# Feed-forward: four intermediate results of each unit stay in PSUM banks instead of SBUF tiles

## The chip, the cores and the metric

The kernel runs on one core of a Trainium2 chip. The core has five engines with a queue each: TensorE (PE in the profile) multiplies matrices into PSUM, VectorE (DVE) and ScalarE (ACT) work element by element on SBUF and PSUM, GpSimd (POOL) works element by element on SBUF, and SyncE (SP) issues the DMAs. An engine takes its instructions in the order in which they stand; engines wait for each other through semaphores. The metric is the time of one execution on the device in microseconds (us), as the median of several runs; lower is better.

## The reference

One layer of a diffusion transformer on 1024 latent tokens of width 1024. The change touches only the last part, the feed-forward, whose inner width is 4096:

```python
def squared_relu_mlp(h, w1, b1, w2, b2):
    return jnp.square(jax.nn.relu(h @ w1 + b1)) @ w2 + b2
...
        hx = modulate(rmsnorm(x_mid, g_norm_mlp[l]), sh2, sc2)
        x = x_mid + gt2 * squared_relu_mlp(hx, w_ff1[l], b_ff1[l], w_ff2[l], b_ff2[l])
```

## The kernel before

Activations are kept with features on the 128 partitions and 512 tokens (one half, `hf` 0 or 1) along a row, so one fp32 tile of 128 x 512 fills one of the eight PSUM banks. For precision every operand of a matmul is split into an upper and a lower part (`hi` by a ScalarE copy, `lo` by a subtraction on VectorE for activations and on GpSimd for weights), and three matmuls make one product.

The 4096 inner rows are worked in 16 units of 256. A unit has two row blocks of 128 and two halves of tokens, hence four hidden tiles: 11 and 12 (first block, token halves 0 and 1), 21 and 22 (second block). From unit 2 on both layers use a seven-product scheme for a 2 x 2 block product. In the first layer (`q_pieces`) the weights of a unit are a11, a12, a21, a22 and the sums s1 to s4 made of them; the token side was combined once before the loop. Seven products, of two pieces each, go in the order a11, a12, s1, s2, s3, s4, a22 into three kinds of banks: `qa` (two buffers), `qb` and `qc` (one each). One unit uses one buffer of each kind. While a bank goes on accumulating, its partial results are taken out: `new` copies a bank into an SBUF tile `ft`, `more` adds a bank to such a tile and applies bias, relu and square (`act`), `begin_21` applies them to the bank qa into a fresh tile. The hidden values come in the order 11, 22, 12, 21.

The second layer (`pair_pieces`) needs the values 11, 22 and 21 and four combinations: t1 = 12 - 11, t3 = 22 - 12, t2 = 22 - t1, t4 = 21 - t2. `sums` makes the first three, `sum_21` the last, each in place in a tile `ft`. `part` (`h_split`) makes the upper and lower parts of each, as `fh` and `fl` or `th` and `tl`. This stretch, from the sum that completes 12 to the last split, is called the tail of a unit here; it occurs in units 2 to 14, 13 times. Unit 15 ends the loop and needs the plain values only.

The products of the second layer go into `fa` (two buffers), `fb` and `fc`, and `add_x` (L1498) adds each, times a gate, to the residual `X`. Within a pair of output blocks the bank `fa` is read twice: after its first product, and again after t2's product has been accumulated onto it.

The order of TensorE, ScalarE, VectorE and GpSimd in the loop is the order in which the code is emitted (`manual_schedule`). `Pieces.emit` walks a list of pieces; it prepares weights `AHEAD` = 5 pieces in advance and puts the `post` functions behind the piece they belong to, or one or more pieces later. The first pieces of the next unit's first layer (a11, both parts, and a12) stand on TensorE between a unit's a22 and its second layer, and so do the tail's instructions on ScalarE and VectorE.

Waits are put in by the framework, from what each instruction reads and writes. Two engines that touch the same PSUM bank are kept apart also when both only read it.

Of the kernel before, what the change touches and what calls it, by code (L numbers as in the profile page):

```python
# [12 lines left out]
ALU = mybir.AluOpType  # L13
# [36 lines left out]
def body(tc, A, out, dbg=None):  # L50
    nc = tc.nc
    V, S, G, PE, SP = nc.vector, nc.scalar, nc.gpsimd, nc.tensor, nc.sync
# [37 lines left out]
    def ps_tile(tag, name, n=512):  # L90
        return cur["pool"].tile([P, n], F32, name=name, tag=tag, bufs=cur["tags"][tag])
# [23 lines left out]
    def CF(name, i=0, n=1):  # L115
        o, w = COLS[name]
        return colf[:, o - NCOLS + 40 + i:o - NCOLS + 40 + i + n]
# [157 lines left out]
    st = ExitStack()  # L275
# [572 lines left out]
    for m in range(2):  # L848
        t = q4("eo")
# [606 lines left out]
    def w_split(a):  # L1456

        n = a.shape[1]
        hi, lo = [wf.tile([P, 2, P], F32R, name=s, tag=s, bufs=6)[:, :n] for s in ("w2h", "w2l")]
        S.activation(hi, a, AF.Copy)  # L1460
        G.tensor_tensor(lo, a, hi.bitcast(F32), ALU.subtract)  # L1461
        return hi, lo

    def w1_load(f, i):
        r = wf.tile([P, 4, P], F32, name="w1r", tag="w1r", bufs=4)
        SP.dma_start(r, A["w_ff1"][f, :, 4 * i:4 * i + 4])
        return r
# [7 lines left out]
    def mm3w(o, w, i, m, start, stop):  # L1475
        for j, (a_, m_) in enumerate(((w[0], m[0]), (w[0], m[1]), (w[1], m[0]))):
            PE.matmul(o, a_[:, i, :], m_, start=start and j == 0, stop=stop and j == 2, skip_group_check=True)  # L1477

    def f_tile():
        return fin.tile([P, H], F32, name="ft", tag="ft", bufs=4)  # L1480

    def act(t, f, src=None):

        S.activation(t, t if src is None else src, AF.Relu, bias=CF("b_ff1", f))  # L1484
        S.activation(t, t, AF.Square)

    def h_split(t, extra=False):
        if extra:
            hi, lo = [th_p.tile([P, H], F32R, name=s, tag=s, bufs=3) for s in ("th", "tl")]
        else:  # L1490
            hi, lo = [fin.tile([P, H], F32R, name=s, tag=s, bufs=4) for s in ("fh", "fl")]
        S.activation(hi, t, AF.Copy)  # L1492
        V.tensor_tensor(lo, t, hi.bitcast(F32), ALU.subtract)  # L1493
        return hi, lo
# [92 lines left out]
    def q_pieces(u):  # L1587

        ts, d = {}, {}
        units[u] = d  # L1590
        st = {}

        def load(i):
            if u + 1 < NU2:
                raws.setdefault(u + 1, []).append(w1_load(2 * u + 2 + i // 2, i % 2))

        def bank(tag):
            if tag not in st:
                st[tag] = ps_tile(tag, tag)
            return st[tag]  # L1600

        def prep(name, h):
            def fn():
                a11, a12, a21, a22 = raws[u]
                if h == 0 and name == "s1":
                    st["ws"] = wf.tile([P, 4, P], F32, name="ws", tag="ws", bufs=1)
                ws = st.get("ws")
                if h == 0:
                    if name == "s1":
                        ES.tensor_tensor(ws, a21, a22, ALU.add)  # L1610
                    elif name == "s2":
                        ES.tensor_tensor(ws, ws, a11, ALU.subtract)
                    elif name == "s3":
                        ES.tensor_tensor(a21, a11, a21, ALU.subtract)  # L1614
                    elif name == "s4":
                        ES.tensor_tensor(ws, a12, ws, ALU.subtract)
                a = {"a11": a11, "a12": a12, "a22": a22, "s3": a21}.get(name, ws)
                w = w_split(a[:, 2 * h:2 * h + 2])
                if h == 0 and name == "s4":
                    for i in range(3):  # L1620
                        load(i)
                if h == 1 and name == "a22":
                    load(3)
                return w
            return fn

        def new(i, bank_):
            ts[i] = f_tile()
            S.copy(ts[i], bank_)  # L1629

        def more(i, bank_, also=None):
            V.tensor_tensor(ts[i], ts[i], bank_, ALU.add)  # L1632
            if also:
                also()
            act(ts[i], 2 * u + i // 20)

        def part(key, i, extra=False):
            d[key] = h_split(ts[i], extra)

        def sums():  # L1640
            V.tensor_tensor(ts[11], ts[12], ts[11], ALU.subtract)
            V.tensor_tensor(ts[12], ts[22], ts[12], ALU.subtract)
            V.tensor_tensor(ts[22], ts[22], ts[11], ALU.subtract)

        def begin_21():
            ts[21] = f_tile()
            act(ts[21], 2 * u + 1, st["qa"])

        def sum_21():
            V.tensor_tensor(ts[21], ts[21], ts[22], ALU.subtract)  # L1650

        post_q1 = (lambda: new(11, st["qa"]),)
        post_q2 = (lambda: more(11, st["qc"]),)
        post_q5 = (lambda: new(22, st["qb"]),)
        post_q6 = (lambda: new(12, st["qa"]),)
        pre_q7 = (lambda: part((0, 0), 11),)
        post_q7 = (lambda: more(22, st["qa"]),)
        if u == NU2 - 1:
            post_q3 = (lambda: more(12, st["qb"]), lambda: part((1, 1), 22), lambda: part((0, 1), 12))
            post_q4 = (begin_21, lambda: part((1, 0), 21))  # L1660
        else:
            post_q3 = (lambda: more(12, st["qb"], lambda: part((1, 1), 22)), sums)
            post_q4 = (lambda: (begin_21(), part("t1", 11)), lambda: (part((1, 0), 21), part("t2", 22, True)),
                       lambda: (sum_21(), part("t3", 12, True)), lambda: part("t4", 21, True))

        def piece(name, tag, b, start, h, post):
            def mm(w):
                o = bank(tag)
                for k in range(2):
                    mm3w(o, w, k, b[2 * h + k], start and h == 0 and k == 0, h == 1 and k == 1)  # L1670
            pc.entry((u, name, h), prep(name, h))
            return lambda: pc.add((u, name, h), mm, post if h == 1 else pre_q7 if name == "s3" else None)

        return [piece(*x[:4], h, x[4]) for x in (
            ("a11", "qa", b11, True, post_q1), ("a12", "qc", b21, True, post_q2), ("s1", "qb", c1, True, post_q5),
            ("s2", "qa", c2, False, post_q6), ("s3", "qa", c3, False, post_q7), ("s4", "qb", b22, False, post_q3),
            ("a22", "qa", c4, False, post_q4)) for h in range(2)]
# [95 lines left out]
    with tc.manual_schedule(engines=MAN):  # L1773
        for u in range(2, NU2):
            q = q_pieces(u)
            for _ in range(4 if u == 2 else 3):
                q.pop(0)()
            (plain_pieces if u == 2 else pair_pieces)(u - 1, q)
            for f in q:
                f()  # L1780
        pc.emit(AHEAD)
# [157 lines left out]
```

## Time and profile before

| | |
|---|---|
| median of 3 runs | 1326.41 us (1323.22 to 1332.71) |
| the profiled execution | 1320.52 us |
| its span, first to last instruction | 1318.4 us |
| TensorE matmuls busy | 1182.3 us, 90% |
| VectorE busy | 1025.8 us, 78% |
| GpSimd busy | 799.6 us, 61% |
| ScalarE busy | 650.7 us, 49% |
| mean granted clock of TensorE | 0.958 of full speed |

A busy share is a mean over the whole execution. Where an engine holds the others up is read from the waits and the timelines, which give for each instruction its start, its length and what ended the idle time ahead of it. Starts in one timeline can overlap a little, since an engine begins an instruction before the last one has quite ended. In the timelines a row with xN stands for N instructions in a row.

### The profile page before, as it was taken

The page shows a single profiled execution, that of the slowest core. Times are in us where ns is not written, and L with a number is a line of the kernel's source. Part 1 is how long each engine was busy: PE and PEld are TensorE (multiplying, and loading weights), DVE is VectorE, ACT ScalarE, POOL GpSimd, SP SyncE. Part 2 cuts the span into 40 slices and gives each one's busy share as a digit, 9 for nine tenths or more (in the row PEclk, how much of TensorE's full clock was granted, in tenths as well). Part 3 has the DMA queues.
Part 4 walks back from the last instruction along what each step waited for, and adds up shares of the span by engine and source line. Part 5 has one row for each costly group of instructions (what it writes and reads, how often), then busy time and mean ns, then how long its engine had stood idle before and what let it go on. Part 6 is the DMA issues. An engine that isn't in the chain of part 4 may idle for free.

```text
span 1318.4 us, 18813 instructions
## 1 busy us (share of the span) xinstructions
PE 1182.3 (90%) x6252; PEld 961.2 (73%) x6252; DVE 1025.8 (78%) x1604; ACT 650.7 (49%) x1335; POOL 799.6 (61%) x1004
## 2 busy tenths in 40 slices
PE   5997888997847889999989999999999999999995
PEld 3775667876636777877778787777877777877775
DVE  4657898599997857669794678888889888788877
ACT  5344334223255646555654454555544555545565
POOL 2147786472556642123566588777877777777764
PEclk9988998998876999999999999999999999999998
DMA  9554341251173554233120111111120111111113
GB/s 347 177 173 147 107 128 54 95 182 40 40 226 95 155 159 112 98 97 112 48 73 33 40 65 57 32 50 55 65 64 33 49 57 56 64 35 46 56 41 128
DMA packets 75058, 121.75 MB, mean 92 GB/s; under 512 B 16977, under 2 KB 35154, under 8 KB 74962
## 3 DMA queue, kind: packets, MB, share of 16 engines
q1 hardware_dynamic: 62802, 113.22, 26.6%
q10 hardware_dynamic: 12160, 7.34, 1.8%
q8 instruction: 49, 0.80, 0.3%
q14 instruction: 47, 0.39, 0.1%
HBM read 106.66 MB, written 13.88 MB: 91 GB/s over the span
## 4 chain that ended last, share of the span: by engine, by line
PE 52%; DVE 27%; ACT 5%; POOL 3%; DMA 3%; issue 3%; SPq 1%; ACTq 0%; DVEq 0%; POOLq 0%
PE fa L1477 11%; PE qa L1477 6%; PE qb L1477 6%; PE fb L1477 5%; DVE cacc L1020 3%; DVE tl L1493 3%; PE fc L1477 2%; PE p_t L1275 2%; PE mm L1102 2%; DVE fl L1493 2%; PE mm L364 2%; PE mm L1477 2%; DVE X L1498 1%; PE p_t L1263 1%; PE f L1477 1%
## 5 line engine op out<-in xcount | busy, mean ns | idle before, releaser
L1461 POOL TENSOR_TENSOR w2l<-w2r,w2h 128x128 fp32r<-128x128 f32 (+1 forms) x232 | 176.8, 763 | 68.8 <-ACT w2h L1460 61.1
L1498 DVE SCALAR_TENSOR_TENSOR X<-fa,gt2c,X 128x512 f32<-128x512 f32 x216 | 159.4, 745 | 13.9 <-PE fa L1477 13.9
L1460 ACT ACTIVATE w2h<-w2r 128x128 fp32r<-128x128 f32 (+1 forms) x232 | 86.1, 388 | 142.7 <-POOL w2r L1711 78.1
L235 POOL TENSOR_TENSOR wlo<-wraw,whi 128x1024 fp32r<-128x1024 f32 x30 | 74.3, 2479 | 124.0 <-ACT whi L233 118.2
L1461 POOL TENSOR_TENSOR w2l<-w1r,w2h 128x256 fp32r<-128x256 f32 x136 | 108.9, 817 | 61.2 <-ACT w2h L1460 34.4
L1498 DVE SCALAR_TENSOR_TENSOR X<-fb,gt2c,X 128x512 f32<-128x512 f32 x108 | 80.5, 745 | 36.5 <-PE fb L1477 36.0
L1461 POOL TENSOR_TENSOR w2l<-ws,w2h 128x256 fp32r<-128x256 f32 x84 | 67.9, 815 | 41.4 <-ACT w2h L1460 41.4
L1020 DVE SCALAR_TENSOR_TENSOR cacc<-cv,wdw,cacc 128x512 f32<-128x512 f32 x92 | 85.1, 971 | 0.4
L1477 PE MATMUL fa<-th,w2h 128*128 128x512 f32 x156 | 63.2, 405 | 19.7 <-DVE X L1498 19.7
L364 PE MATMUL mm<-xh,whi 128*128 128x512 f32 x192 | 77.1, 418 | 3.6 <-ACT xh L218 2.7
L364 PE MATMUL mm<-xl,whi 128*128 128x512 f32 x192 | 78.9, 411 | 0.5 <-DVE xl L220 0.5
L1460 ACT ACTIVATE w2h<-w1r 128x256 fp32r<-128x256 f32 x136 | 54.1, 410 | 48.7 <-DVE w1r L1614 19.1
L364 PE MATMUL mm<-xh,wlo 128*128 128x512 f32 x192 | 77.8, 407 | 0.0
L1477 PE MATMUL qa<-cb,w2h 128*128 128x512 f32 x224 | 70.6, 396 | 0.7 <-ACT ft L1629 0.7
L1493 DVE TENSOR_TENSOR fl<-ft,fh 128x512 fp32r<-128x512 f32 x64 | 56.1, 893 | 11.9 <-ACT fh L1492 11.3
L1477 PE MATMUL fa<-th,w2l 128*128 128x512 f32 x156 | 61.4, 394 | 0.8 <-POOL w2l L1461 0.8
L1477 PE MATMUL fa<-tl,w2h 128*128 128x512 f32 x156 | 61.5, 394 | 0.0
L1018 POOL TENSOR_TENSOR pacc<-pacc,ptmp 128x512 f32<-128x512 f32 x24 | 41.0, 1708 | 25.4 <-ACT ptmp L1017 25.4
L1460 ACT ACTIVATE w2h<-ws 128x256 fp32r<-128x256 f32 x84 | 33.2, 411 | 41.4 <-DVE ws L1610 20.7
L1477 PEld LDWEIGHTS fa<-th,w2h 128*128 128x128 f32 x156 | 29.3, 188 | 31.0 <-DVE X L1498 25.2
L1477 PEld LDWEIGHTS qa<-cb,w2h 128*128 128x128 f32 x224 | 42.0, 188 | 11.3 <-ACT ft L1629 1.1
L1484 ACT ACTIVATE ft<-ft,colf 128x512 f32<-128x512 f32 x42 | 30.5, 727 | 35.4 <-DVE ft L1632 35.4
(787 smaller groups left out, 3893.0 us busy)
## 6 DMA issues: line engine op xcount, KB each, us to landing
w2r<-in_w_ff SPq DMA_DIRECT2D x68, 256.0 KB
wmB<-in_wmodB SPq DMA_DIRECT2D x32, 512.0 KB
w1r<-in_w_ff SPq DMA_DIRECT2D x64, 256.0 KB
wm<-in_wmodA SPq DMA_DIRECT2D x16, 512.0 KB
wraw<-in_w_in SPq DMA_DIRECT2D x12, 512.0 KB
x<-in_xT SPq DMA_DIRECT2D x8, 512.0 KB
wraw<-in_w_out SPq DMA_DIRECT2D x8, 512.0 KB
kr<-k_d SPq DMA_DIRECT2D x16, 256.0 KB
```

The costliest lines, as they stand in the source:

```text
L235: (lo_eng or G).tensor_tensor(lo, raw, hi.bitcast(F32), ALU.subtract)
L364: PE.matmul(o, a_[:, k, :], b_[hf][k], start=k == 0 and i == 0, stop=k == 7 and i == 2)
L1018: G.tensor_tensor(pacc, pacc, t, ALU.add)
L1020: V.scalar_tensor_tensor(acc, x(k), w(k), acc, ALU.mult, ALU.add)
L1102: PE.matmul(o, a_[:, 2 * kk + c, :], b_, start=c == 0 and i == 0, stop=c == 1 and i == 2)
L1275: PE.matmul(po[:, j * 64:j * 64 + 64], ptt[:, i * P:(i + 1) * P], rv, start=i == 0, stop=i == 4, skip_group_check=True)
L1460: S.activation(hi, a, AF.Copy)
L1461: G.tensor_tensor(lo, a, hi.bitcast(F32), ALU.subtract)
L1477: PE.matmul(o, a_[:, i, :], m_, start=start and j == 0, stop=stop and j == 2, skip_group_check=True)
L1484: S.activation(t, t if src is None else src, AF.Relu, bias=CF("b_ff1", f))
L1493: V.tensor_tensor(lo, t, hi.bitcast(F32), ALU.subtract)
L1498: return V.scalar_tensor_tensor(x, o, gt2(k), x, ALU.mult, ALU.add).ins
```

## The change

Three results stay in the unit's own banks, and a fourth value is made in one:

- `more(12, ..., keep=True)`: the sum that completes value 12 is written back into the bank qb, and relu and square run in place there; later t3 takes its place in qb.
- `sums`: the first difference, t1, is written into the bank qc, which has been empty since value 11 took its content.
- `begin_21`: relu and square of value 21 run in place in the bank qa; later t4 takes its place in qa.

Unit 15 keeps its 12 in SBUF, and only its 21 in the bank.

```diff
-        def more(i, bank_, also=None):
-            V.tensor_tensor(ts[i], ts[i], bank_, ALU.add)
+        def more(i, bank_, also=None, keep=False):
+
+            t, ts[i] = ts[i], bank_ if keep else ts[i]
+            V.tensor_tensor(ts[i], t, bank_, ALU.add)
             if also:
                 also()
             act(ts[i], 2 * u + i // 20)
...
         def sums():
-            V.tensor_tensor(ts[11], ts[12], ts[11], ALU.subtract)
+            V.tensor_tensor(st["qc"], ts[12], ts[11], ALU.subtract)
+            ts[11] = st["qc"]
             V.tensor_tensor(ts[12], ts[22], ts[12], ALU.subtract)
             V.tensor_tensor(ts[22], ts[22], ts[11], ALU.subtract)

         def begin_21():
-            ts[21] = f_tile()
-            act(ts[21], 2 * u + 1, st["qa"])
+            ts[21] = st["qa"]
+            act(ts[21], 2 * u + 1)
...
-            post_q3 = (lambda: more(12, st["qb"], lambda: part((1, 1), 22)), sums)
+            post_q3 = (lambda: more(12, st["qb"], lambda: part((1, 1), 22), True), sums)
```

Line numbers behind `more` move by two or three. On VectorE the tail keeps its order, and the operands change. The difference of the two programs at the tail of unit 2 (- before, + changed):

```order
-L1632 TENSOR_TENSOR ft<-ft,qa 128x512
-L1632 TENSOR_TENSOR ft<-ft,qb 128x512
-L1493 TENSOR_TENSOR fl<-ft,fh 128x512
-L1641 TENSOR_TENSOR ft<-ft 128x512
-L1642 TENSOR_TENSOR ft<-ft 128x512
-L1643 TENSOR_TENSOR ft<-ft 128x512
+L1634 TENSOR_TENSOR ft<-ft,qa 128x512
+L1634 TENSOR_TENSOR qb<-ft,qb 128x512
+L1493 TENSOR_TENSOR fl<-ft,fh 128x512
+L1643 TENSOR_TENSOR qc<-qb,ft 128x512
+L1645 TENSOR_TENSOR qb<-ft,qb 128x512
+L1646 TENSOR_TENSOR ft<-ft,qc 128x512
```

L1641 to L1643 become L1643, L1645 and L1646, one for one; nothing moves. On ScalarE, in the same tail (`w2h` are upper parts of weights for later pieces):

```order
-L1484 ACTIVATE ft<-ft,colf 128x512
-L1485 ACTIVATE ft<-ft 128x512
-L1460 ACTIVATE w2h<-w2r 128x256
-L1460 ACTIVATE w2h<-w1r 128x256
-L1484 ACTIVATE ft<-qa,colf 128x512
+L1484 ACTIVATE qb<-qb,colf 128x512
+L1485 ACTIVATE qb<-qb 128x512
+L1460 ACTIVATE w2h<-w2r 128x256
+L1460 ACTIVATE w2h<-w1r 128x256
+L1484 ACTIVATE qa<-qa,colf 128x512
+L1485 ACTIVATE qa<-qa 128x512
+L1492 ACTIVATE fh<-qc 128x512
```

Relu and square of 12 and 21 keep their places; the upper half of t1 is now read from qc. The one place where the order differs is TensorE right behind the loop, where the last unit's second layer begins and the framework sets the order (`f_...` are its result tiles, `c_...` the parts of its weights). Before:

```order
L1477 MATMUL f_12483<-fh,c_12462 128x512
L1477 MATMUL f_12492<-fh,c_12462 128x512
L1477 MATMUL f_12503<-fh,c_12466 128x512
L1477 MATMUL f_12483<-fl,c_12462 128x512
L1477 MATMUL f_12483<-fh,c_12463 128x512
```

Changed:

```order
L1477 MATMUL f_12469<-fh,c_12448 128x512
L1477 MATMUL f_12469<-fl,c_12448 128x512
L1477 MATMUL f_12469<-fh,c_12449 128x512
L1477 MATMUL f_12469<-fh,c_12448 128x512
L1477 MATMUL f_12469<-fl,c_12448 128x512
```

Two products with an upper half that stood ahead of the first one with a lower half now come behind it.

## Rows read from the trace of the kernel before

**Rows 1.** the page, the chain that ended last, shares of the span by engine.

```profile
PE 52%; DVE 27%; ACT 5%; POOL 3%; DMA 3%; issue 3%; SPq 1%; ACTq 0%; DVEq 0%; POOLq 0%
```

**Rows 2.** TensorE's waits, 740 to 1275 us: line, line waited for, total, times, longest.

```profile
PE fa L1477 <- DVE X L1498: 19.7, 13, 1.5
```

**Rows 3.** busy time in a stretch: us, then engines, granted clock, DMA share, GB/s.

```profile
958.64:999.07 40.43, 38.91 (x169) 31.49 (x169) 33.76 (x47) 21.31 (x49) 31.21 (x47) 1.00 0.17 53
```

**Rows 4.** TensorE's timeline: start us, us, engine, line, operation, [idle before it <-releaser].

```profile
992.40 0.39 PE L1477 MATMUL qa<-mh,w2l 128*128 128x512 f32 x1
992.63 0.39 PE L1477 MATMUL qc<-mh,w2h 128*128 128x512 f32 x1
...
997.16 0.39 PE L1477 MATMUL fb<-fh,w2l 128*128 128x512 f32 x1
999.07 0.50 PE L1477 MATMUL fa<-th,w2h 128*128 128x512 f32 x1 [1.52 <-DVE X L1498]
999.40 0.39 PE L1477 MATMUL fa<-tl,w2h 128*128 128x512 f32 x1
...
999.86 0.63 PE L1477 MATMUL qb<-c,w2h 128*128 128x512 f32 x2
```

**Rows 5.** VectorE's timeline through one unit's tail.

```profile
987.39 0.69 DVE L1632 TENSOR_TENSOR ft<-ft,qb 128x512 f32<-128x512 f32 x1 [2.04 <-PE qb L1477]
987.99 1.15 DVE L1493 TENSOR_TENSOR fl<-ft,fh 128x512 fp32r<-128x512 f32 x1
989.54 0.69 DVE L1641 TENSOR_TENSOR ft<-ft 128x512 f32<-128x512 f32 x1 [0.39 <-ACT ft L1485]
990.27 1.11 DVE L1642 TENSOR_TENSOR ft<-ft 128x512 f32<-128x512 f32 x1
991.41 0.84 DVE L1643 TENSOR_TENSOR ft<-ft 128x512 f32<-128x512 f32 x1
992.17 1.82 DVE L1493 TENSOR_TENSOR fl<-ft,fh 128x512 fp32r<-128x512 f32 x2
993.91 1.23 DVE L1493 TENSOR_TENSOR tl<-ft,th 128x512 fp32r<-128x512 f32 x1
995.06 1.22 DVE L1650 TENSOR_TENSOR ft<-ft 128x512 f32<-128x512 f32 x1
996.20 1.55 DVE L1493 TENSOR_TENSOR tl<-ft,th 128x512 fp32r<-128x512 f32 x2
997.67 0.68 DVE L1610 TENSOR_TENSOR ws<-w1r 128x512 f32<-128x512 f32 x1
998.27 0.74 DVE L1498 SCALAR_TENSOR_TENSOR X<-fa,gt2c,X 128x512 f32<-128x512 f32 x1
```

**Rows 6.** GpSimd's timeline, in the tail and behind it.

```profile
990.79 0.91 POOL L1709 TENSOR_TENSOR w2r<-w2r 128x128 f32<-128x128 f32 x1
...
1002.11 0.46 POOL L1709 TENSOR_TENSOR w2r<-w2r 128x128 f32<-128x128 f32 x1
```

**Rows 7.** instructions on the tile X, 900 to 1000 us: ns min/median/max.

```profile
L1498 DVE SCALAR_TENSOR_TENSOR X<-fa,gt2c,X x35: 733/744/752, 900.3 to 998.3; 128x512 f32<-128x512 f32 x35
```

**Rows 8.** VectorE's groups by shape: count, busy us, mean ns, idle before.

```profile
L1632 DVE TENSOR_TENSOR ft<-ft,qb 128x512 f32<-128x512 f32 x14 | 9.6, 687 | 28.7 <-PE qb L1477 28.7
...
L1512 DVE TENSOR_TENSOR cv<-cv,ml 128x512 f32<-128x512 f32 x8 | 5.5, 695 | 0.0
```

**Rows 9.** ScalarE's timeline in the same tail.

```profile
988.11 0.73 ACT L1484 ACTIVATE ft<-ft,colf 128x512 f32<-128x512 f32 x1 [0.19 <-DVE ft L1632]
988.87 0.64 ACT L1485 ACTIVATE ft<-ft 128x512 f32<-128x512 f32 x1
...
990.11 0.69 ACT L1484 ACTIVATE ft<-qa,colf 128x512 f32<-128x512 f32 x1
```

**Rows 10.** ScalarE's groups by shape.

```profile
L1460 ACT ACTIVATE w2h<-w1r 128x256 fp32r<-128x256 f32 x136 | 54.1, 410 | 48.7 <-DVE w1r L1614 19.1 <-PE qa L1477 8.7 <-PE f L1477 7.1
...
L1519 ACT ACTIVATE c<-cv 128x512 fp32r<-128x512 f32 x8 | 4.8, 599 | 2.5 <-DVE cv L1517 2.5
```

## The prediction

> **What bounds the kernel now.** I read the chain that ended last first: TensorE holds 52% of it and VectorE 27% [rows 1]. So VectorE matters wherever TensorE waits for it, and nowhere else. The list of TensorE's waits over the feed-forward loop then has one entry that counts: 13 times, once in each of 13 units, a matmul on bank `fa` waits for a residual add, 1.5 us each [rows 2]. [...]
>
> TensorE's timeline shows what a wait takes. Matmuls start 0.23 us apart (992.40, 992.63). One starts at 997.16, the next only at 999.07, and the one behind it 0.33 us later [rows 4]. The loss is 1.91 - 0.23 = 1.68, and 0.33 - 0.23 = 0.10 for the slow restart: 1.78 us a unit, 13 x 1.78 = 23.1 us in all. That is the most this change can win.
>
> VectorE's timeline shows why. The add that TensorE wants (998.27) stands in VectorE's queue behind the whole unit tail: the third value's sum (987.39), the differences L1641 to L1643, the lower halves of the splits, L1650, and the next unit's weight sum L1610 [rows 5]. From 989.54 on it hardly rests. Its rows for one shape differ: 0.69 at L1641, 1.11 at L1642, 0.84 at L1643, 1.23 and 1.22 further down. GpSimd's rows stretch in the same place: L1709 takes 0.91 at 990.79, and 0.46 at 1002.11, when VectorE does residual adds [rows 6]. Those adds read one operand from PSUM and stay within 733 to 752 ns while GpSimd works beside them [rows 7]. So I read the long rows as a price of VectorE reading two SBUF operands while GpSimd reads SBUF, and one PSUM operand as free of it.
>
> **What the change does, part by part.** No instruction is added or removed, and ScalarE, VectorE and GpSimd keep their order in the loop. What changes is where operands live. In each of 13 tails eight VectorE instructions that now have two SBUF operands get one in PSUM: L1641, L1642, L1643, L1650 and four of the six split halves. Two keep two SBUF operands (the halves of (1, 1) and of t2).
>
> Prices. VectorE from PSUM into PSUM: `cv<-cv,ml` 695 ns, from PSUM into SBUF: the present sum 687 [rows 8]. I take 0.69 for all. ScalarE from PSUM: 0.69 with a bias (L1484 from qa), 0.60 without (L1519 from cv), against 0.73 and 0.64 from SBUF [rows 9, 10]. ScalarE writing PSUM has no row; I take the same as writing SBUF and bound it below.
>
> [...] By the rows above, an add with an operand in PSUM takes 687 ns and L1641, which reads SBUF alone and begins while GpSimd rests, 0.69: no difference. [...]
>
> The tail again with these prices, on the clock of the unit shown. An instruction without a wait starts 0.09 before the last one ends (987.39 + 0.69, next at 987.99); one that waits starts 0.03 after its releaser (988.11 behind 988.08) [rows 5, 9].
> Sum 987.39 to 988.08. Relu 988.11 to 988.80, square to 989.43 (now 989.51). First difference into qc 989.46 to 990.15; the second into qb 990.06 to 990.75; the third 990.79 to 991.48 (now it ends at 992.25). ScalarE's upper half of qc: now it runs as soon as the first difference is there and ScalarE is free. In the changed program it waits for VectorE's third difference, which only reads that bank too. So 991.51 to 992.11; ScalarE's own queue (the fourth value's relu from 990.11, 0.69, and square, 0.60) would have held it until 991.43 anyway, so this wait costs 0.08. Lower half from qc 992.14 to 992.83.
>
> **The wait that is added.** The bank `qc` is now taken from the first difference to that lower half. The next unit's a12 product writes it at 992.63 [rows 4]. It must now wait until 992.83 + 0.06 = 992.89 (0.06 lies between the add's end, 999.01, and TensorE's restart, 999.07): 0.26, and 0.10 for the restart, 0.36 a unit. All of TensorE's queue stands behind it, so the later matmul arrives at 997.39 + 0.36 = 997.75. The bank qb is next written at 999.86 [rows 4], after its last read, and qa has a second buffer: these wait for nothing. In the last unit only the fourth value stays in its bank, which nothing else wants.
>
> VectorE goes on: lower half from qa 992.74 to 993.43; t2's half (two SBUF operands) 993.34 to 994.03, or to 994.57 at 1.23; L1650 to 994.63 or 995.17; ScalarE's upper half of t4 to 995.26 or 995.80; the last lower half to 995.98 or 996.52; L1610 to 996.57 or 997.11; the add to 997.23 or 997.77, and TensorE could go on at 997.29 or 997.83. It arrives at 997.75. So the old wait is gone but for 0.08 at most, and what is late next is `qc`.
>
> Saved per unit: 1.78 - 0.36 = 1.42; 13 x 1.42 = 18.5 us. At the end of the program four first matmuls stand in another order, and two that fill a wait today come behind it: at most 2 x 0.23 = 0.46 lost. **Sum: 18.0 us.** The profiled execution, 1320.5, would become 1302.5; it lies 5.9 under the median of the runs, so the median goes from 1326.4 to **1308.4**.
>
> **Bounds.** The unknown is ScalarE's write into PSUM, twice on the path (relu, square). A half-width row takes 0.41 [rows 10], a full one 0.64, so the fixed part of an instruction is about 2 x 0.41 - 0.64 = 0.18. If PSUM adds that once more to each, the lower half ends 0.36 later, a unit saves 1.06, the sum is 13.3 and the time 1313.1. If it takes it away, the lower half ends before 992.57 and `qc` waits for nothing: the whole 23.1 - 0.46 = 22.7 is won, 1303.7. No row leans to either end, so I stay at zero.
>
> **Rivals.**
> 1. *The whole stall goes*, 1303.7: ScalarE on PSUM is quicker by 0.13 or more per instruction. For: it reads PSUM 0.03 to 0.04 quicker [rows 9, 10]; against: that is a fourth of what is needed. [...]
> 2. *The bank is held longer*, 1313 and up: ScalarE on PSUM is dearer by 0.18 or more, or something in the new chain sum, relu, square, difference, split waits longer. Each 0.1 per ScalarE instruction takes 13 x 0.2 = 2.6 us. At 0.71 each the gain is zero, beyond that the kernel is slower.
> 3. *VectorE's rows stay long*, slower: if 1.11, 0.84, 0.91, 1.23 and 1.22 belong to the place and not to the second SBUF operand, the split of qc, which now follows the third difference, runs from 992.70 to 993.61, `qc` costs 1.14, and the add ends at 999.34, TensorE going on at 999.40 and not 999.07: 13 x 0.33 + 0.46 = 4.8 more, 1331.2. It decides once the add ends later than 999.01. Against it stand the adds of [rows 7] and GpSimd's two rows [rows 6].
> That the change does nothing can be excluded: the built program has the operands in the banks.
>
> **How the numbers follow.** Forecast 0.66; rival 1 0.17; rival 2 0.12; rival 3 0.04; 0.01 for what I do not see. One per cent, 13.3 us, is about what a measurement of this kernel can tell from no change (the runs shown spread over 9.5), so faster means under 1313.1. Faster: 0.66 + 0.17 = 0.83, less 0.02 for a forecast that comes out at its dear end; same: rival 3, rival 2 but for 0.01, and that 0.02, together 0.17; slower: the rest, 0.02. The range runs from 1303.7 and 1313.1 outward by some 2.5 us on each side, for the scatter of the median.
>
> **What will show it.** In the trace of after: L1645 and L1646 at 0.69 and no 1.1; L1709 in the tail near 0.5; TensorE's wait for the add at `fa` gone, and in its place 13 short waits at `qc` for L1493, about 0.3 each; the stretch from unit to unit 39.0 us. I am wrong if ScalarE's L1484 and L1485 on qb take over 0.8 each, if the add still ends the wait, or if weight preparation on GpSimd becomes what TensorE waits for.

## The result and the profile after

The changed kernel takes **1307.43 us** (median of 6 runs, 1304.56 to 1311.16); the kernel before took 1326.43 beside it (6 runs, 1323.22 to 1336.01). The ratio is 0.984 with a 95% interval of 0.9809 to 0.9871. Forecast were 1308.4 and a range of 1301.2 to 1315.6. The profiled execution took 1304.56, its span 1302.6 against 1318.4.

The chain that ended last, from the page of the changed kernel (shares of the span), answers to [rows 1]:

```profile
PE 57%; DVE 21%; ACT 6%; DMA 4%; issue 3%; POOL 3%; SPq 0%; ACTq 0%; DVEq 0%; POOLq 0%
```

VectorE fell from 27% to 21% of it. The list of TensorE's waits over the feed-forward loop, 735 to 1265 us (line, line waited for, total, times, longest), answers to [rows 2]:

```profile
PE f L1477 <- ACT fh L1492: 1.6, 1, 1.6
PE fa L1477 <- POOL w2l L1461: 0.7, 1, 0.7
PE qa L1477 <- ACT ft L1629: 0.7, 1, 0.7
PE f L1477 <- DVE fl L1493: 0.3, 1, 0.3
```

The 13 waits for the residual add, 19.7 us together, are gone; each row left is a single wait. VectorE's timeline through the same tail (start us, us, engine, line, operation, idle before it) answers to [rows 5]. To compare the two, add 7.06 us to its times (987.39 - 980.33):

```profile
980.33 0.70 DVE L1634 TENSOR_TENSOR qb<-ft,qb 128x512 f32<-128x512 f32 x1 [2.06 <-PE qb L1477]
980.93 1.14 DVE L1493 TENSOR_TENSOR fl<-ft,fh 128x512 fp32r<-128x512 f32 x1
982.37 0.70 DVE L1643 TENSOR_TENSOR qc<-qb,ft 128x512 f32<-128x512 f32 x1 [0.30 <-ACT qb L1485]
982.97 0.69 DVE L1645 TENSOR_TENSOR qb<-ft,qb 128x512 f32<-128x512 f32 x1
983.69 0.69 DVE L1646 TENSOR_TENSOR ft<-ft,qc 128x512 f32<-128x512 f32 x1
985.05 0.69 DVE L1493 TENSOR_TENSOR fl<-qc,fh 128x512 fp32r<-128x512 f32 x1 [0.67 <-ACT fh L1492]
...
986.25 0.68 DVE L1493 TENSOR_TENSOR tl<-ft,th 128x512 fp32r<-128x512 f32 x1
986.85 0.69 DVE L1653 TENSOR_TENSOR qa<-qa,ft 128x512 f32<-128x512 f32 x1
...
988.21 0.69 DVE L1493 TENSOR_TENSOR tl<-qa,th 128x512 fp32r<-128x512 f32 x1
988.82 0.68 DVE L1610 TENSOR_TENSOR ws<-w1r 128x512 f32<-128x512 f32 x1
989.41 0.74 DVE L1498 SCALAR_TENSOR_TENSOR X<-fa,gt2c,X 128x512 f32<-128x512 f32 x1
```

Rows that took 1.11, 0.84, 1.23 and 1.22 take 0.68 to 0.70 now. The add that TensorE wanted ends at 990.15, on the old clock 997.21, where it ended at 999.01. Two splits still read two SBUF tiles. One is the only long row left (1.14, at 980.93, while GpSimd works); the other is the row that took 1.23, `tl<-ft,th` at 986.25, and it is short although both its operands are in SBUF: GpSimd, which begins 0.15 behind it, is the one that takes longer there. GpSimd's timeline shows the other side ([rows 6]); L1712 is the old L1709:

```profile
983.43 0.46 POOL L1712 TENSOR_TENSOR w2r<-w2r 128x128 f32<-128x128 f32 x1
...
986.40 1.14 POOL L1461 TENSOR_TENSOR w2l<-w2r,w2h 128x256 fp32r<-128x256 f32 x1 [0.73 <-ACT w2h L1460]
```

Where it took 0.91 it takes 0.46. It is held up only at 986.40, beside that split at 986.25, the last row of this tail with two SBUF operands.

The wait that was added shows on TensorE's timeline ([rows 4]):

```profile
985.34 0.39 PE L1477 MATMUL qa<-mh,w2l 128*128 128x512 f32 x1
985.79 0.50 PE L1477 MATMUL qc<-mh,w2h 128*128 128x512 f32 x1
986.13 0.39 PE L1477 MATMUL qc<-ml,w2h 128*128 128x512 f32 x1
...
990.47 0.39 PE L1477 MATMUL fb<-fh,w2l 128*128 128x512 f32 x1
990.69 0.40 PE L1477 MATMUL fa<-th,w2h 128*128 128x512 f32 x1
```

The first matmul on `qc` starts 0.45 after the one ahead of it, not 0.23, and the next 0.34 after that, not 0.23: 0.33 us a unit. At `fa`, where the gap was 1.91, the matmuls follow at 0.22. The list above does not name the new wait, since the trace puts it on the weight load ahead of the matmul (PEld); the view of all work on the tile `qc` does (who waited for it: us, times):

```profile
  PEld qc L1477: 6.3, 13
```

One unit, from this restart to the next (us, then the engines' busy time, granted clock, DMA share, GB/s), answers to [rows 3]:

```profile
946.77:985.79 39.02, 38.96 (x168) 31.46 (x168) 31.22 (x47) 20.90 (x49) 29.27 (x46) 1.00 0.19 55
```

It is 39.02 us long, of which TensorE is busy 38.96, against 40.43 and 38.91.

### The profile page after: what moved, and what is told of

The parts are those of the page before. It is cut to its first block, busy times and chain, and to the rows that moved or that the text cites. A ratio compares the mean times of both kernels' runs of the same rounds, so it can differ in the third digit from the quotient of the medians.

```text
span 1302.6 us, 18800 instructions
## 1 busy us (share of the span) xinstructions
PE 1184.6 (91%) x6252; PEld 962.1 (74%) x6252; DVE 1003.8 (77%) x1604; ACT 645.0 (50%) x1335; POOL 767.1 (59%) x1004
## 4 chain that ended last, share of the span: by engine, by line
PE 57%; DVE 21%; ACT 6%; DMA 4%; issue 3%; POOL 3%; SPq 0%; ACTq 0%; DVEq 0%; POOLq 0%
PE fa L1477 12%; PE qa L1477 6%; PE fb L1477 6%; PE qb L1477 6%; DVE cacc L1020 3%; PE qc L1477 3%; PE fc L1477 3%; PE p_t L1275 2%; PE mm L1102 2%; PE mm L1477 2%; PE f L1477 1%; DMA kr<-k_d 1%; PE p_t L1263 1%; DVE fl L1493 1%; PE mm L364 1%
## 5 line engine op out<-in xcount | busy, mean ns | idle before, releaser
L1461 POOL TENSOR_TENSOR w2l<-w2r,w2h 128x128 fp32r<-128x128 f32 (+1 forms) x232 | 174.1, 752 | 78.0 <-ACT w2h L1460 71.8
L1461 POOL TENSOR_TENSOR w2l<-w1r,w2h 128x256 fp32r<-128x256 f32 x136 | 102.2, 766 | 65.2 <-ACT w2h L1460 41.3
L1460 ACT ACTIVATE w2h<-w1r 128x256 fp32r<-128x256 f32 x136 | 54.0, 410 | 51.0 <-DVE w1r L1614 19.7
L364 PEld LDWEIGHTS mm<-xh,whi 128*128 128x128 f32 x192 | 38.2, 201 | 17.5 <-ACT xh L218 5.3
L233 ACT ACTIVATE whi<-wraw 128x1024 fp32r<-128x1024 f32 x30 | 31.7, 1056 | 31.9 <-DMA wraw<-in_w_out 10.6
L1498 DVE SCALAR_TENSOR_TENSOR X<-fc,gt2c,X 128x512 f32<-128x512 f32 x56 | 41.9, 749 | 6.9 <-PE fc L1477 2.4
```

Source lines behind the costliest of these rows:

```text
L233: S.activation(hi, raw, AF.Copy)
L364: PE.matmul(o, a_[:, k, :], b_[hf][k], start=k == 0 and i == 0, stop=k == 7 and i == 2)
L1498: return V.scalar_tensor_tensor(x, o, gt2(k), x, ALU.mult, ALU.add).ins
```

## The experiments

All numbers per unit are from the first matmul on `qb` to that of the next unit, 13 such periods; the usual one is 40.45 before and 39.02 after. "The loop" is their sum: 527.9 us before (741.71 to 1269.65) and 509.3 after (743.22 to 1252.55). The wait at `fa` is given from start to start, as in the prediction; TensorE's list of waits shows 0.16 less (1.52 against 1.68). The expectations come from a replay of the rows under an assumption of the author's: VectorE's instructions with two SBUF operands and GpSimd's run one at a time. The rivals to it are that the long rows belong to their place, and that the gain comes from ScalarE's quicker relu and square in PSUM.

**One part of the change alone.** Three kernels keep one result in its bank and put the others back into SBUF tiles. Against the changed kernel, the first:

```diff
-            V.tensor_tensor(st["qc"], ts[12], ts[11], ALU.subtract)
-            ts[11] = st["qc"]
+            V.tensor_tensor(ts[11], ts[12], ts[11], ALU.subtract)
...
-            ts[21] = st["qa"]
-            act(ts[21], 2 * u + 1)
+            ts[21] = f_tile()
+            act(ts[21], 2 * u + 1, st["qa"])
```

The second, with t1 alone in `qc`:

```diff
-            ts[21] = st["qa"]
-            act(ts[21], 2 * u + 1)
+            ts[21] = f_tile()
+            act(ts[21], 2 * u + 1, st["qa"])
...
-            post_q3 = (lambda: more(12, st["qb"], lambda: part((1, 1), 22), True), sums)
+            post_q3 = (lambda: more(12, st["qb"], lambda: part((1, 1), 22)), sums)
```

The third, with 21 alone in `qa`, has the first hunk of the first and the last hunk of the second.

12 alone in `qb`. 

> One part alone: value 12 (later t3) stays in qb; t1 and 21 are SBUF tiles as before. Theory (VectorE's instructions with two SBUF operands and GpSimd's instructions run one at a time in the tail, and the residual add behind the tail sets TensorE's restart): L1642 and the first difference come down to 0.69, the others stay long; replayed with the rows of before, the wait of the add shrinks by about 0.45 us a unit, 5.9 us in all, no wait at qc. Rival (the gain comes from ScalarE's quicker relu and square on PSUM, 0.13 us a unit): 1.7 us. Rival (the long rows belong to the place): no row shorter, 0 to 2 us.

t1 alone in `qc`. 

> One part alone: t1 is written into qc; 12 and 21 are SBUF tiles as before. Theory: the third difference and the lower half of t1 come down to 0.69, the others stay long; the lower half of t1 is ready late, so TensorE waits about 1.0 us at qc and 0.3 at the add: 6.6 us faster than before. Rival (the bank's wait is the only thing this part brings, and the long rows stay): slower than before by 4 us. Rival (ScalarE): no gain, since relu and square stay in SBUF.

21 alone in `qa`. 

> One part alone: 21 (later t4) stays in qa; 12 and t1 are SBUF tiles as before. Theory: the lower halves of 21 and t4 and L1653 come down to about 0.69 in the part of the tail where VectorE has no slack left, and nothing waits for qa: 1.14 us a unit, 14.9 us faster. Rival (ScalarE): relu and square of 21 are off the path, about 0. Rival (place): 0.

Medians on the same chip, the kernel before at 1326.59: 12 alone 1322.8 (ratio 0.9973, 0.9951 to 0.9994), t1 alone 1319.52 (0.9943, 0.9915 to 0.9971), 21 alone 1307.93 (0.9851, 0.9795 to 0.9907). The units take 40.24, 40.00 and 39.39. TensorE's lists of waits, which count matmuls, have one repeated entry each. 12 alone:

```profile
PE fa L1477 <- DVE X L1498: 16.1, 13, 1.2
```

t1 alone:

```profile
PE qc L1477 <- DVE fl L1493: 9.3, 13, 0.7
```

21 alone:

```profile
PE fa L1477 <- DVE X L1498: 5.4, 13, 0.4
```

With t1 alone the matmul at `fa` is late too, by 0.15 to 0.19 from start to start and 0.10 for the restart; the trace puts that wait on the weight load, so the list leaves it out. Both waits that were expected, 1.0 and 0.3, are there: 0.87 + 0.11 at `qc` and this one. The order and the places of the waits are as that assumption says, and ScalarE is not the gain: with t1 alone its relu and square of 12 and 21 write SBUF tiles as before, and 0.45 a unit is saved. But 12 alone saves 0.21 a unit and not 0.45. Its VectorE timeline shows where the rest went, rows of one tail:

```profile
998.58 0.75 DVE L1645 TENSOR_TENSOR ft<-ft 128x512 f32<-128x512 f32 x1
999.84 2.05 DVE L1493 TENSOR_TENSOR fl<-ft,fh 128x512 fp32r<-128x512 f32 x2 [0.51 <-ACT fh L1492]
1001.81 1.23 DVE L1493 TENSOR_TENSOR tl<-ft,th 128x512 fp32r<-128x512 f32 x1
```

The differences are short, but the two splits behind them, which still read SBUF alone, take 2.05 where they took 1.82 [rows 5]; the author reads this as GpSimd's work meeting the next two-SBUF row. Keeping t1 in `qc` brings the wait at `qc`, which is longer here than in the whole change (0.87 from start to start), since relu and square of 12 write SBUF (the first difference starts 2.14 behind the sum that completes 12, in the whole change 2.04) and L1645 takes 1.10 (there 0.69), so the bank is released later. The gains do not add: 0.21 + 0.45 + 1.06 = 1.72 a unit for the parts, 1.43 for the whole.

**Without t1.** The cause of the new wait taken away: 12 and 21 stay in their banks, t1 goes into SBUF.

```diff
-            V.tensor_tensor(st["qc"], ts[12], ts[11], ALU.subtract)
-            ts[11] = st["qc"]
+            V.tensor_tensor(ts[11], ts[12], ts[11], ALU.subtract)
```

> The change without the part that takes qc: 12 in qb, 21 in qa, t1 in an SBUF tile. Theory: no wait at qc, the residual add is done 0.2 us before TensorE wants it, all 23 us of the stall are won, 4 us more than with the change: about 1303. Rival (t1 in PSUM is needed to shorten VectorE's queue enough): the wait at the add comes back with 0.3 us or more a unit, the time is that of the change or above, 1307 to 1312.

1309.44 (1300.47 to 1312.57; ratio 0.9853, 0.9796 to 0.9911), and not the expected 1303. No matmul starts late at `qc` or at `fa`; the unit takes 38.80, the loop 506.2. But the add is done just in time, not 0.2 ahead: the weight load on `fa` still waits 0.26 for it, once a unit, as the list of the weight loads' waits shows:

```profile
PEld fa L1477 <- DVE X L1498: 3.4, 13, 0.3
```

The matmul behind the first one on `fa` then comes 0.11 late, so this restart is what is left of the 1.78. The changed kernel had not run beside it, so both were run again, on one chip.

> The change without the part that takes qc, beside the change on the same chip. Theory: 38.83 a unit against 39.02, 13 times: 2.5 us under the change, near what can be told. Rival (the loop's gain is given back behind it): no difference.

> The change itself, as the measure for the other two on the same chip: 39.02 a unit, 1307.

Without t1: 1303.19 (1298.2 to 1307.61; 0.9843, 0.9804 to 0.9882). The change: 1310.79 (1303.69 to 1319.56; 0.9895, 0.9858 to 0.9932). The kernel before took 1325.39 there. The loops took 504.9 and 509.4. In this second profile of the change `qc` again costs 0.33 in every unit, but the median unit takes 39.23, against the 39.02 that was expected: in 6 of its 13 units a weight load waits some 0.3 for a later residual add (in the first profile in 2), and matmuls there come up to 0.1 late. The loops come out equal all the same, since one unit of the first profile took 40.31. One unit of the kernel without t1 (windows, columns as above):

```profile
944.00:982.80 38.80, 38.80 (x170) 31.42 (x169) 31.77 (x46) 20.90 (x48) 29.67 (x47) 1.00 0.18 54
```

In this row TensorE counts as busy throughout; the 0.11 is hidden in it. In its loop this version is 3.1 to 4.5 us quicker than the change in every profile. That it is quicker as a whole is likely and not settled: the medians differ by 7.6 on one chip and by 2.0 the other way across two, and the intervals overlap.

**GpSimd's work taken away.** The kernel before, in which GpSimd does not make the combinations of the second layer's weights; this part of the computation is left out, and the products use the weights as they are.

```diff
-                    w = w_split({"a": t[:, 0:2], "b": t[:, 0:5:4], "c": t[:, 1:3], "d": t[:, 3:4]}[name])
-                    if name == "a":
-                        EP.tensor_tensor(t[:, 4], t[:, 2], t[:, 3], ALU.add)
-                        EP.tensor_tensor(t[:, 2], t[:, 0], t[:, 2], ALU.subtract)
-                        EP.tensor_tensor(t[:, 0], t[:, 4], t[:, 0], ALU.subtract)
-                    elif name == "b":
-                        EP.tensor_tensor(t[:, 1], t[:, 1], t[:, 0], ALU.subtract)
+                    w = w_split({"a": t[:, 0:2], "b": t[:, 0:4:3], "c": t[:, 1:3], "d": t[:, 3:4]}[name])
```

> The kernel before, all operands in SBUF, without GpSimd's four combinations of second-layer weights per output pair (L1709 to L1711, L1713); the products then take uncombined weights, so this part of the computation is left out. Nothing of VectorE, ScalarE or TensorE is changed. Theory (VectorE's two-SBUF instructions and GpSimd's run one at a time): L1643 and the lower halves behind it come down from 0.84 to 0.91 towards 0.69, the wait at the add shrinks by about 0.9 us a unit, the unit from 40.45 to 39.5. Rival (the long rows belong to the place in the tail): rows and wait as before, 40.45.

1311.3 against 1324.77 (ratio 0.991, 0.9881 to 0.994); the unit takes 39.57. VectorE's rows in one tail, with all operands in SBUF as before:

```profile
996.27 1.12 DVE L1643 TENSOR_TENSOR ft<-ft 128x512 f32<-128x512 f32 x1
997.31 1.28 DVE L1493 TENSOR_TENSOR fl<-ft,fh 128x512 fp32r<-128x512 f32 x2
998.51 1.23 DVE L1493 TENSOR_TENSOR tl<-ft,th 128x512 fp32r<-128x512 f32 x1
999.66 0.68 DVE L1650 TENSOR_TENSOR ft<-ft 128x512 f32<-128x512 f32 x1
```

And GpSimd's:

```profile
995.65 1.19 POOL L1461 TENSOR_TENSOR w2l<-w1r,w2h 128x256 fp32r<-128x256 f32 x1
998.44 0.75 POOL L1461 TENSOR_TENSOR w2l<-w2r,w2h 128x256 fp32r<-128x256 f32 x1 [1.60 <-ACT w2h L1460]
```

The same instructions are long where GpSimd works and short where it rests: the two splits at 997.31 take 1.28 together, not 1.82, and L1650 takes 0.68, not 1.22. L1643 was expected to come down and went up, 1.12 against 0.84: GpSimd's `w2l` of 995.65 now meets it. So the rival that the long rows belong to their place falls.

**The bank released one split later.** The changed kernel with the split of 21 ahead of that of t1:

```diff
-            post_q4 = (lambda: (begin_21(), part("t1", 11)), lambda: (part((1, 0), 21), part("t2", 22, True)),
+            post_q4 = (lambda: (begin_21(), part((1, 0), 21), part("t1", 11)), lambda: part("t2", 22, True),
```

> The change, with the split of 21 ahead of the split of t1 on ScalarE and VectorE, so that qc is read last one split later. Theory (the release of qc by the lower half of t1 is what TensorE now waits for, and the add has slack): the wait at qc grows from 0.33 to about 0.85 us, the unit from 39.02 to 39.55, 6.8 us slower than the change, 12 faster than before. Rival (the wait at qc is hidden behind the later add, or the add is still next): the unit stays at 39.0 to 39.1.

1315.0 against 1324.77 (ratio 0.9936, 0.9911 to 0.9962), the unit 39.55, as expected. Its list of TensorE's waits:

```profile
PE qc L1477 <- DVE fl L1493: 7.8, 13, 0.6
```

From start to start the wait at `qc` is 0.76 and the restart 0.10, against 0.22 and 0.11 in the changed kernel: 0.53 more, and the unit is 0.53 longer. So it is the release of `qc` that TensorE waits for.

**The wait taken away by order alone.** If a wait at the add is the whole loss, the kernel before should gain as much when the tail's last splits, t3 and t4, and the sum L1650 between them are emitted three pieces later, behind that add:

```diff
+                       lambda: None, lambda: None, lambda: None,
                        lambda: (sum_21(), part("t3", 12, True)), lambda: part("t4", 21, True))
```

> The kernel before, all operands in SBUF, with L1650 and the splits of t3 and t4 put behind the residual add that TensorE waits for. Theory (what costs is where the add stands in VectorE's queue; shorter rows are one way to bring it forward): the add is done at 996.9 on the clock of before, TensorE does not wait, the unit takes 38.7, 23 us faster than before: about 1303. Rival (the tail must be shorter, since the moved splits make the next matmul on t3 wait instead): the wait comes back at the matmul on t3, 40 or more a unit, 0 to 6 us faster.

1382.33 against 1324.77 (ratio 1.0452, 1.0425 to 1.0478): the expectation failed. The wait at `fa` did go, and another came. TensorE's timeline (first row) and, behind it, VectorE's and ScalarE's:

```profile
990.65 0.77 PE L1477 MATMUL fb<-fh,w2h 128*128 128x512 f32 x1 [4.31 <-DVE X L1498]
```

```profile
988.49 0.69 DVE L1493 TENSOR_TENSOR tl<-ft,th 128x512 fp32r<-128x512 f32 x1 [1.97 <-ACT th L1492]
...
989.76 0.74 DVE L1498 SCALAR_TENSOR_TENSOR X<-fb,gt2c,X 128x512 f32<-128x512 f32 x1
```

```profile
986.55 0.72 ACT L1484 ACTIVATE ft<-ft,colf 128x512 f32<-128x512 f32 x1 [2.29 <-DVE ft L1632]
...
987.84 0.61 ACT L1492 ACTIVATE th<-ft 128x512 fp32r<-128x512 f32 x1
```

Read from the bottom: the upper half of t4 now stands on ScalarE behind relu and square of the next unit's value 11, which wait for VectorE. VectorE's lower half of t4 waits for that upper half, and the adds that empty `fc` and `fb` stand behind it. TensorE waits 4.31 us, and a unit takes 44.5 to 46.1. TensorE is slow afterwards, too (windows, columns as in [rows 3]):

```profile
986.30:990.60 4.30, 0.04 (x1) 0.00 (x0) 2.33 (x5) 2.38 (x5) 1.68 (x3) 0.92 0.00 0
990.60:994.00 3.40, 3.35 (x8) 2.71 (x9) 1.73 (x3) 1.14 (x3) 3.21 (x7) 0.50 0.30 77
...
997.00:998.00 1.00, 1.00 (x6) 0.81 (x5) 0.80 (x2) 0.00 (x0) 0.54 (x2) 1.00 0.00 0
```

**Only the lower halves late.** To avoid that, the upper halves stay early where they can, and the lower halves go where VectorE has room; `upper` and `lower` are the two lines of `h_split`, emitted apart:

```diff
-                       lambda: (sum_21(), part("t3", 12, True)), lambda: part("t4", 21, True))
+                       lambda: upper("t3", 12), none, none, none, none, none, lambda: lower("t3", 12),
+                       lambda: (sum_21(), upper("t4", 21)), none, lambda: lower("t4", 21))
```

> The kernel before, all operands in SBUF, with t3's lower half, L1650 and t4's split behind those residual adds that TensorE wants next, and with the upper halves ahead of ScalarE's relu of the next unit's first value. Theory (the cost is where the adds that TensorE waits for stand in VectorE's queue; the bank is one way to bring them forward, an order by need another): no wait at the first add, at most 0.2 us at the third, the unit takes 38.7 to 38.9, some 20 us faster than before. Rival (the tail is too much work for VectorE with long rows, in whatever order): a wait of 1 us or more at another add, 39.7 or more a unit.

1313.47 against 1325.39 (ratio 0.9919, 0.9886 to 0.9951), the unit 39.42: 12 us faster and not the expected 20. The wait at the first add is all but gone; a weight load still waits for it, and the matmul behind comes 0.09 late. The list of TensorE's waits has one new entry, which neither theory had:

```profile
PE fa L1477 <- ACT w2h L1460: 5.5, 13, 0.4
```

ScalarE's timeline names what that weight part waits for, GpSimd's combination L1720:

```profile
996.41 0.42 ACT L1460 ACTIVATE w2h<-w2r 128x256 fp32r<-128x256 f32 x1 [1.09 <-POOL w2r L1720]
```

GpSimd's own rows there, three combinations in a row:

```profile
993.98 0.99 POOL L1718 TENSOR_TENSOR w2r<-w2r 128x128 f32<-128x128 f32 x1
995.05 0.46 POOL L1719 TENSOR_TENSOR w2r<-w2r 128x128 f32<-128x128 f32 x1
995.59 0.79 POOL L1720 TENSOR_TENSOR w2r<-w2r 128x128 f32<-128x128 f32 x1
```

They take 0.99 and 0.79 where VectorE's late two-SBUF instructions now run (L1650 at 993.98, a lower half at 995.35), and 0.46 between them. Order alone saves 1.03 us a unit, with all results in SBUF; the price of two SBUF operands moves to GpSimd, and the weights are what is late next.

## Why the prediction was right

**The bound.** Right. The 1.78 us a unit at `fa` came from VectorE's long tail: they are gone from the list of waits after, and two kernels that shorten or reorder that tail without any bank, by less work on GpSimd and by the lower halves put late, save 0.88 and 1.03 a unit.

**VectorE's prices.** 0.69 was taken for all. The groups of after have 679 ns (`tl<-qb,th`) to 699 (L1643). The last add was to end between 997.23 and 997.77 on the old clock; it ended at 997.21. That the rows shrink because one operand comes from PSUM while GpSimd reads SBUF is shown from both sides, by the change and by GpSimd's work taken away: L1650, which took 1.22 [rows 5], takes 0.69 as L1653 with an operand in `qa`, and 0.68 with both in SBUF where GpSimd rests, in the kernel with less work on it. The PSUM operand brought no visible price of its own: these rows take 679 to 699 ns, and L1610, which reads SBUF alone while GpSimd rests, takes 681.

**The added wait.** Forecast 0.26 and 0.10 for the restart, measured 0.22 and 0.11. The lower half that releases `qc` ended at 985.74, on the old clock 992.80; forecast was 992.83. ScalarE's part, from the timeline of after:

```profile
981.06 0.66 ACT L1484 ACTIVATE qb<-qb,colf 128x512 f32<-128x512 f32 x1 [0.23 <-DVE qb L1634]
981.75 0.58 ACT L1485 ACTIVATE qb<-qb 128x512 f32<-128x512 f32 x1
...
983.74 0.58 ACT L1485 ACTIVATE qa<-qa 128x512 f32<-128x512 f32 x1
984.41 0.60 ACT L1492 ACTIVATE fh<-qc 128x512 fp32r<-128x512 f32 x1
```

ScalarE was free at 984.32 and began the split of qc 0.03 behind VectorE's third difference, which ends at 984.38: the wait between two readers of one bank cost 0.09, forecast 0.08. Both count from the end of ScalarE's last instruction; by the prediction's own rule an instruction that waits for nothing starts 0.09 before that, so the true cost is about 0.18 and the forecast should have been 0.17. The sum is untouched by this, since it goes by the start itself.

**Rival 1** had the sign right and too much size. Its mechanism is there: in place in PSUM relu takes 662 ns and square 582, in SBUF 724 and 633 (means of after's groups by shape, in the loop). The sum had put relu at 0.69 and square at 0.60 and needed 0.13 less each for `qc` to wait for nothing; it got 0.02 to 0.03. Of relu's 62 ns the write is the smaller part: from the bank `qa` it takes 690 ns into SBUF, in the kernel before, and 661 back into the bank, 29 less. **Rival 2** did not come about; the kernel with the later release shows that its mechanism is real, 0.53 us a unit for one more split. **Rival 3** fell with the short rows and with GpSimd's work taken away.

**The sum.** 1.42 a unit was forecast, 1.43 measured (40.45 - 39.02). The loop saved 527.9 - 509.3 = 18.6, forecast 18.5.

**The end.** At most 0.46 was to be lost behind the loop. From the last first matmul on `qb` to the end it is 50.1 us after and 48.8 before, 1.3 more. The reordered matmuls cost 0.47 of this, as forecast: from the first matmul on `f` to the sixteenth it is 4.18 after and 3.71 before, since nothing covers the second of these waits now (TensorE's timeline of after):

```profile
1259.78 0.51 PE L1477 MATMUL f<-fh,c 128*128 128x512 f32 x1 [1.60 <-ACT fh L1492]
1260.58 0.50 PE L1477 MATMUL f<-fl,c 128*128 128x512 f32 x1 [0.30 <-DVE fl L1493]
```

The other 0.8 lies behind TensorE's last matmul, where the output is finished and stored: from its start to the end 8.06 after and 7.28 before. The sum put nothing there. In the profiles of all these kernels this stretch takes either 7.27 to 7.29 or 8.03 to 8.06, and no run settles why. Ahead of the loop, where the program is the same, after was 1.5 later (743.2 against 741.7); the start of the loop lies anywhere from 741 to 753 in these profiles. So the profiled execution saved 1320.52 - 1304.56 = 16.0 us and not 18.0, while the medians, 19.0 apart, came out 1.0 under the forecast. The agreement of the total to 1 us is partly luck, and so is that of the unit to 0.01, since the second profile of the change has a median unit of 39.23. The terms are not luck: in all 26 units of the two profiles the wait at the first add is gone and `qc` costs 0.33, forecast 0.36.

**What the parts are worth** the prediction did not ask. 21 in `qa` alone gives three quarters of the gain of a unit (1.06 of 1.43), and t1 in `qc` takes 0.22 away again.

## What to carry to other kernels

When VectorE's rows of one shape differ in length (here 0.69 to 1.23), look at what GpSimd does at the same moment and at how many operands come from SBUF: a bank that stands idle anyway can be the place for one of them (here eight rows a tail then took 0.68 to 0.70). Cost the release of that bank like any other wait: its readers, in their order, against the matmul that writes it next; a part of a change that holds a bank too long can be left out (here t1). Moving work behind the instruction that is waited for can make something else late by more (here 4.31 us, where the old wait was 1.52): follow each half of a moved step on its own engine. And where a list of matmul waits is empty, read the weight loads' waits too: here they held the new wait at `qc` (6.3 us in all) and, without t1, what was left of the old one (3.4).

## What the runs showed of the hardware

- **Idle time and clock.** TensorE idle for 1.52 us kept a granted clock of 1.00 [rows 3, 4], and the unit of the changed kernel without that wait has 1.00 as well: closing the gap gave no clock back. After it was idle for 4.31 us, in the kernel with t3 and t4 moved, the granted clock was 0.50 from 990.60 to 994.00, and 1.00 again from 997.00. The 14 steps from matmul to matmul between 990.65 and 996.76 took 6.11 us and not 14 x 0.23 = 3.2, so the clock cost 2.9 us on top of the wait in this unit, one of the longest (46.0 us).
- **ScalarE in place in PSUM** is 51 to 62 ns quicker per 128x512 instruction than in SBUF (relu 662 against 724 ns, square 582 against 633).
- **Who pays.** In two places where a two-SBUF row of VectorE met GpSimd's `w2l`, the price fell on the one that began later. In the changed kernel that was GpSimd: 1.14 at 986.40, beside VectorE's 0.68 from 986.25 on. In the kernel with less work on GpSimd it was VectorE: 1.23 at 998.51, beside GpSimd's 0.75 from 998.44 on.
